# Attention block: the low parts of three value weights computed by VectorE, the other weights still by an adding DMA

## The chip, the cores and the metric

One core of one Trainium2 chip runs the whole kernel. The metric is the device time of one execution in microseconds, as the median of several runs. The engines are called here as in the profile: PE is TensorE (matmuls), PEld its weight loads, DVE is VectorE, ACT is ScalarE, POOL is GpSimd, SP is SyncE, which issues the loads.

## The reference, cut to what matters

One layer of a hybrid backbone over 512 latent and 256 context tokens of width 1024, in float32. Three branches (a gated linear recurrence, differential attention, a gated MLP) read one input projection, are gated, merged and normalised. The change lies in the attention branch, in the projection that gives the values:

```python
px = split_proj(modulate(x, sh_x, sc_x), w_in[l], b_in[l])
...
vx = px[4].reshape(B, T, DIFF_HEADS, DIFF_V_DIM)
k_all = jnp.concatenate([kx, kc], axis=1)
v_all = jnp.concatenate([vx, vc], axis=1)
...
s = jnp.einsum('bqhmd,bkhmd->bhmqk', q.astype(f32), k.astype(f32)) * (DIFF_HEAD_DIM ** -0.5)
p = jax.nn.softmax(s, axis=-1)
w = p[:, :, 0] - lam * p[:, :, 1]
return jnp.einsum('bhqk,bkhe->bqhe', w, v.astype(f32)).astype(v.dtype)
```

There are 8 heads with values of 128 channels each.

## The kernel before, in words

**Split operands.** TensorE multiplies in a rounded float32 format. Each operand is therefore kept as a high part (the value rounded to that format) and a low part (value minus high part), and every product is three matmuls, high by high, high by low and low by high (lines 62, 63 and 64, in `mm3`).

**Weights.** A list `pieces` fixes the order in which 512 KB pieces of weights are loaded and split. SyncE loads a piece into one of three `raw` buffers (`w_dma`). `w_conv` then casts it to the high part on ScalarE (line 133) and makes the low part. In the first and last stages (`state["lo"]` names an engine) VectorE subtracts (line 138). During attention `state["lo"]` is None: ScalarE writes the negated piece, minus `raw`, to the low tile (line 135), and GpSimd issues a DMA that adds the high part's source on top (line 136), so that the low part is what the rounding left over. A raw buffer is free for the next load when its last reader is through.

**Kinds of weights.** Kind `"cm"` is a 128-column block in one piece (keys, queries, gates). Kind `"tm"` is a pair of heads' values, 256 columns in two pieces of 512 rows each, with separate tiles for the high part and the low part. During attention there are three of kind tm: w10, w15 and w20, for head pairs 1, 2 and 3. The pair 0 (w4) is split before attention begins. The names in the rows are these numbers: w15h and w15l are the high and low part of weight 15, raw15_0 and raw15_1 its two pieces.

**Attention.** A loop over 32 steps i, four blocks of 128 queries for each of eight heads. Step i does `scores(i)` (line 729, two matrices s_0 and s_1 in two of three large PSUM buffers), `softmax(i)` (row maxima by VectorE, line 739; exponentials by ScalarE, line 744; a scaling by ScalarE, line 747), and `combine(i)` (VectorE, line 754: the two softmaxes are combined, and the PSUM buffer of s_1 is read for the last time). The transposes of step i-1 (line 759) and their split into wth (ScalarE, line 770) and wtl (VectorE, line 772) follow, and once per head the product with the values (o, lines 62 to 64). Between these, projections for later heads fill TensorE: one projection per step, as written in the table `fill`. The value projections of pair p are the groups v_0 to v_5, one token block of 128 each; their results are split into vh (ScalarE, line 54) and vl (VectorE, line 55).

**Order.** TensorE's instructions stand in the order in which the code is written. The other engines' instructions are put in order by a scheduler that estimates when each can run, and on each engine they run strictly in that order. The first value group of w15 follows the scores of step 13, that of w20 the scores of step 21, that of w10 the scores of step 5.

Of the kernel before, what the change touches and what calls it, by code (L numbers as in the profile page):

```python
# [13 lines left out]
ALU = mybir.AluOpType  # L14
# [15 lines left out]
def block_kernel(ctx, tc, x, c, cctx_in, c_ctx, w_ada, b_ada, w_in, b_in, conv_w, conv_b,  # L30
# [4 lines left out]
    V, S, G, PE = nc.vector, nc.scalar, nc.gpsimd, nc.tensor  # L35

    def f(ap):
        return ap.bitcast(F32)
# [43 lines left out]
    reqs, pieces, raws, parts, last = [], [], {}, {}, {}  # L82
    state = {"dma": 0, "conv": 0, "use": 0, "lo": G, "keep": None, "slot": 0}
# [14 lines left out]
    def w_dma():  # L98
        if state["dma"] >= len(pieces):
            return  # L100
        i, part = pieces[state["dma"]]
        kind, src, c0 = reqs[i][:3]
        if kind == "cm":
            raw = wp.tile([P, KT, P], F32, tag="raw", bufs=3, name=f"raw{i}")
            nc.sync.dma_start(raw, src[:, c0:c0 + P].rearrange("(k p) c -> p k c", p=P))
        elif kind != "tm":
            raw = wp.tile([P, 2, 512], F32, tag="raw", bufs=3, name=f"raw{i}_{part}")
            r0 = 512 * int(kind[1]) + 256 * part
            nc.sync.dma_start(raw, src[r0:r0 + 256, c0:c0 + 512]
                              .rearrange("(k p) c -> p k c", p=P))  # L110
        else:
            raw = wp.tile([P, KT // 2, CW], F32, tag="raw", bufs=3, name=f"raw{i}_{part}")
            nc.sync.dma_start(raw, src[part * 512:part * 512 + 512, c0:c0 + CW]
                              .rearrange("(k p) c -> p k c", p=P))
        raws[state["dma"]] = raw
        state["dma"] += 1

    def w_conv(ahead=True):
        j = state["conv"]
        i, part = pieces[j]  # L120
        kind, slots = reqs[i][0], reqs[i][3]
        if kind == "cm":
            t = wp.tile([P, 2, KT, P], F32R, tag=f"w{slots[0]}", bufs=1, name=f"w{i}")
            parts[i] = (t[:, 0], t[:, 1])
            h, l = parts[i]
        else:
            if part == 0:
                dims = [P, KT, CW] if kind == "tm" else [P, 4, 512]
                parts[i] = tuple(wp.tile(dims, F32R, tag=f"w{sl}", bufs=1, name=f"w{i}{n}")
                                 for sl, n in zip(slots, "hl"))  # L130
            n = parts[i][0].shape[1] // 2
            h, l = (t[:, n * part:n * part + n] for t in parts[i])
        state["hi"] = S.copy(h, raws[j])  # L133
        if state["lo"] is None:
            S.mul(l, raws[j], -1.0)
            G.dma_start(f(l), raws[j], accum_op=ALU.add)  # L136
        else:
            state["lo"].tensor_tensor(l, raws[j], f(h), ALU.subtract)  # L138
        state["conv"] += 1
        if ahead:  # L140
            w_dma()

    def pump(n=1):
        for _ in range(n):
            if state["conv"] >= len(pieces):
                return
            i, part = pieces[state["conv"]]
            if part == 0 and not all(retired(x) for x in reqs[i][4]):
                return
            w_conv()  # L150

    def w_next():
        i = state["use"]
        state["use"] += 1
        while state["conv"] < len(pieces) and pieces[state["conv"]][0] <= i:
            w_conv()
        return parts[i]
# [110 lines left out]
    with tc.tile_pool(name="hd", bufs=1) as hd:  # L268
# [43 lines left out]
        w_dma()  # L312
        state["lo"] = V
        w_conv()
        state["lo"] = G
        load_ada(1)
# [1010 lines left out]
```

## Time and profile before

| | before |
|---|---|
| median of 3 runs | 1010.98 us (1009.31 to 1011.77) |
| the profiled execution's own time | 1007.99 us |
| its span | 1006.2 us |
| TensorE busy, share of the span | 959.5 us, 95% |
| VectorE busy | 629.2 us, 63% |
| ScalarE busy | 553.2 us, 55% |
| GpSimd busy | 107.4 us, 11% |
| mean granted TensorE clock | 0.983 of full speed |

The span is the time from the first to the last instruction in the profile, 1.8 us less than the execution's own time. Busy shares are averages over stages that have different limits; TensorE's 95% still leaves 46.7 us in which it does nothing. The attention loop lies between about 84 and 372 us of the span.

### The profile page before, as it was taken

To read this page: it belongs to the slowest core of one execution; us is meant where nothing else is said; L and a number is where in the kernel's file an instruction comes from. 1 tells how busy PE (TensorE), PEld (TensorE's weight loads), DVE (VectorE), ACT (ScalarE), POOL (GpSimd) and SP (SyncE) were. 2 spreads that over 40 slices of the span, in tenths; PEclk is the share of its full clock that TensorE was granted. 3 is DMA by queue.
4 is the path that set the end of the run, shared out by engine and by line. 5 is a ranking of instruction groups with operands and counts; after the bars stand their busy time and mean duration, and the time that the engine had idled before them with its cause. 6 is when DMAs were issued, how large, how long until landed. Compare 5 with 4: busy or idle time off the path is not lost.

```text
span 1006.2 us, 13286 instructions
## 1 busy us (share of the span) xinstructions
PE 959.5 (95%) x5239; PEld 813.1 (81%) x5239; DVE 629.2 (63%) x996; ACT 553.2 (55%) x771; POOL 107.4 (11%) x118
## 2 busy tenths in 40 slices
PE   5999899989979989999999999999999999999995
PEld 4797779879869868878888887788888888888885
DVE  4468759759758653788778775477333366325566
ACT  4168866757757797998777796333221143332221
POOL 2132122212212121100000000000000000000002
PEclk8999999989989999999999999999999999999998
DMA  9937453362271275222332223734323322845212
GB/s 313 303 101 173 92 139 72 71 152 63 61 170 42 64 159 126 82 74 85 105 94 84 84 76 101 254 109 142 93 75 109 101 84 84 277 140 167 86 41 84
DMA packets 147316, 119.08 MB, mean 118 GB/s; under 512 B 4109, under 2 KB 133622, under 8 KB 147254
## 3 DMA queue, kind: packets, MB, share of 16 engines
q1 hardware_dynamic: 140790, 95.85, 31.5%
q0 software_dynamic: 6320, 22.29, 10.9%
q8 instruction: 41, 0.67, 0.3%
q14 instruction: 21, 0.17, 0.0%
q10 hardware_dynamic: 144, 0.10, 0.0%
HBM read 94.10 MB, written 4.19 MB: 98 GB/s over the span
## 4 chain that ended last, share of the span: by engine, by line
PE 74%; ACT 9%; DVE 9%; DMA 4%; issue 3%; SPq 0%; POOL 0%; POOLq 0%; ACTq 0%; DVEq 0%
PE y L62 4%; PE y L64 4%; PE y L63 4%; PE gt L62 4%; PE gt L64 4%; PE gt L63 4%; PE s L729 3%; DMA raw<-in_w_in_dram 2%; PE out L63 2%; PE out L62 1%; PE out L64 1%; PE v L63 1%; PE gc L62 1%; PE gc L64 1%; PE gc L63 1%
## 5 line engine op out<-in xcount | busy, mean ns | idle before, releaser
L133 ACT CAST w<-raw 128x1024 fp32r<-128x1024 f32 x96 | 99.8, 1044 | 89.6 <-PE y L64 25.3
L138 DVE TENSOR_TENSOR w<-raw,w 128x1024 fp32r<-128x1024 f32 x71 | 86.8, 1229 | 75.2 <-ACT w L133 75.2
L62 PE MATMUL gt<-xhl,w 128*128 128x512 f32 x192 | 75.5, 393 | 0.0
L64 PE MATMUL gt<-xhl,w 128*128 128x512 f32 x192 | 74.8, 390 | 0.0
L63 PE MATMUL gt<-xhl,w 128*128 128x512 f32 x192 | 74.8, 390 | 0.0
L739 DVE TENSOR_REDUCE mxn<-s 128x1 f32<-128x768 f32 x64 | 58.3, 950 | 5.3 <-PE s L729 5.2
L729 PE MATMUL s<-kd,qdq 128*128 128x512 f32 (+1 forms) x256 | 55.6, 358 | 3.0 <-issue 2.8
L729 PEld LDWEIGHTS s<-kd,qdq 128*128 128x128 f32 x256 | 42.9, 191 | 12.7 <-issue 6.3
L62 PEld LDWEIGHTS gt<-xhl,w 128*128 128x128 f32 x192 | 36.1, 188 | 7.6
L64 PEld LDWEIGHTS gt<-xhl,w 128*128 128x128 f32 x192 | 36.0, 188 | 7.7
L63 PEld LDWEIGHTS gt<-xhl,w 128*128 128x128 f32 x192 | 36.1, 188 | 7.1
L744 ACT ACTIVATE e<-s,mxn 128x768 f32<-128x768 f32 x32 | 28.8, 899 | 18.0 <-DVE mxn L739 17.9
L754 DVE SCALAR_TENSOR_TENSOR e<-s,sm,e 128x768 f32<-128x768 f32 x32 | 32.6, 1018 | 7.9 <-ACT e L747 7.1
L1208 POOL PARTITION_BROADCAST grb<-grs x8 | 3.8, 581 | 296.7 <-DVE grs L1205 296.7
L54 ACT CAST vh<-v 128x128 fp32r<-128x128 f32 x48 | 12.3, 265 | 40.5 <-PE v L64 17.8
L772 DVE TENSOR_TENSOR wtl<-t,wth 128x768 fp32r<-128x768 f32 x32 | 30.4, 952 | 6.3 <-ACT wth L770 6.1
L866 ACT ACT_TABLE_LOAD x25 | 32.1, 1283 | 0.4
L747 ACT ACTIVATE e<-e,sm 128x768 f32<-128x768 f32 x32 | 29.9, 936 | 0.4 <-DVE sm L746 0.4
L136 POOL DMA_DIRECT2D w<-raw x24 | 21.5, 907 | 77.0 <-PE s L729 34.3
L866 ACT ACTIVATE rt<-ri,colB 128x770 f32<-128x770 f32 x32 | 28.1, 905 | 2.5 <-PE ri L64 1.4
L744 ACT ACTIVATE s<-s,mxn 128x768 f32<-128x768 f32 x32 | 27.8, 868 | 0.5 <-DVE mxn L739 0.5
L971 POOL DMA_DIRECT2D pa_d<-ha x8 | 4.4, 550 | 220.4 <-DVE ha L970 220.4
(463 smaller groups left out, 3029.2 us busy)
## 6 DMA issues: line engine op xcount, KB each, us to landing
raw<-in_w_in_dram SPq DMA_DIRECT2D x96, 512.0 KB, 4.2
w<-raw POOLq DMA_DIRECT2D x24, 512.0 KB, 4.8
raw<-in_w_branch_dram SPq DMA_DIRECT2D x24, 512.0 KB, 4.0
ada<-in_w_ada_dram SPq DMA_DIRECT2D x6, 1024.0 KB, 8.7
qdq<-qdq POOLq DMA_DIRECT2D x16, 256.0 KB, 5.6
adg<-in_w_ada_dram SPq DMA_DIRECT2D x8, 512.0 KB, 6.3
raw<-in_w_out_dram SPq DMA_DIRECT2D x8, 512.0 KB, 3.6
xtok<-in_x_dram SPq DMA_DIRECT2D x4, 512.0 KB, 5.6
```

The lines of the kernel that those rows point to most:

```text
L62: PE.matmul(ps, ah, bh, start=(first and i == 0), stop=False)
L63: PE.matmul(ps, ah, bl, start=False, stop=False)
L64: PE.matmul(ps, al, bh, start=False, stop=(last and i == n - 1))
L133: state["hi"] = S.copy(h, raws[j])
L138: state["lo"].tensor_tensor(l, raws[j], f(h), ALU.subtract)
L729: PE.matmul(sp[:, sl], qds[h][:, 2 * m + j, qs], kds[h][:, m, sl], start=(j == 0), stop=(j == 1))
L739: V.tensor_reduce(mxn[:, m:m + 1], sps[m][:, 0:TA], mybir.AxisListType.X, ALU.max, negate=True)
L744: S.activation(e, sps[m][:, 0:TA], AF.Exp, bias=mxn[:, m:m + 1], accum_out=sm[:, m:m + 1])
L747: S.mul(es[i][0], es[i][0], sm[:, 0:1])
L754: V.scalar_tensor_tensor(e0, e1, sm[:, 1:2], e0, op0=ALU.mult, op1=ALU.add)
L772: V.tensor_tensor(wts[h][1][:, :, qs], src, f(wts[h][0][:, :, qs]), ALU.subtract)
L866: order[0] = S.activation(out, in_, fn, **kw)
```

## The change

For weights of kind tm during attention, the low part is computed by VectorE as raw minus high part, in one instruction for each piece. Kind cm keeps the negated copy and the adding DMA.

```diff
         state["hi"] = S.copy(h, raws[j])
-        if state["lo"] is None:
+        if state["lo"] is None and kind == "tm":
+            V.tensor_tensor(l, raws[j], f(h), ALU.subtract)
+        elif state["lo"] is None:
             S.mul(l, raws[j], -1.0)
             G.dma_start(f(l), raws[j], accum_op=ALU.add)
         else:
```

This concerns six pieces, two of each of w10, w15 and w20. ScalarE loses six instructions (688 rows of order become 682), GpSimd six DMAs, VectorE gains six. The lines below the change are numbered two higher afterwards (754 becomes 756), and the new instruction is line 135. TensorE's and SyncE's orders keep the same instructions; some of their waits differ.

VectorE's order at step 12, before. The names: s12 and s13 are scores, sm12 the sums, mxn13 the negated maxima, e0_12 the combined softmax, t11 the transposed one, v1_5 the last value group of pair 1, zq4 and t1q4 the query of head 4 on its way through the rotation.

```order
L739 TENSOR_REDUCE mxn12_1956<-s12_1_1950 128x1
L594 TENSOR_TENSOR kd4_1856<-zc4_1888,kd4_1856 64x256
L746 RECIPROCAL sm12_1955<-sm12_1955 128x1
L594 TENSOR_TENSOR kd4_1856<-zc4_1888,kd4_1856 64x256
L55 TENSOR_TENSOR vl2_1300<-v1_5_1904,vh2_1299 128x128
L752 RECIPROCAL sm12_1955<-sm12_1955 128x1
L753 TENSOR_TENSOR sm12_1955<-sm12_1955,nlam_87 128x1
L754 SCALAR_TENSOR_TENSOR e0_12_1958<-s12_1_1950,sm12_1955,e0_12_1958 128x768
L55 TENSOR_TENSOR vl3_1368<-v1_5_1904,vh3_1367 128x128
L545 STREAM_SHUFFLE t1q4_2009<-zq4_1998 128x512
```

The same place of VectorE's order in the changed kernel:

```order
L741 TENSOR_REDUCE mxn12_1952<-s12_1_1946 128x1
L596 TENSOR_TENSOR kd4_1854<-zc4_1886,kd4_1854 64x256
L748 RECIPROCAL sm12_1951<-sm12_1951 128x1
L596 TENSOR_TENSOR kd4_1854<-zc4_1886,kd4_1854 64x256
L55 TENSOR_TENSOR vl2_1298<-v1_5_1902,vh2_1297 128x128
L135 TENSOR_TENSOR w15l_1932<-raw15_0_1400,w15h_1931 128x1024
L754 RECIPROCAL sm12_1951<-sm12_1951 128x1
L55 TENSOR_TENSOR vl3_1366<-v1_5_1902,vh3_1365 128x128
L755 TENSOR_TENSOR sm12_1951<-sm12_1951,nlam_87 128x1
L135 TENSOR_TENSOR w15l_1932<-raw15_1_1622,w15h_1931 128x1024
L756 SCALAR_TENSOR_TENSOR e0_12_1954<-s12_1_1946,sm12_1951,e0_12_1954 128x768
L547 STREAM_SHUFFLE t1q4_2005<-zq4_1994 128x512
```

Both low parts, and vl3, now stand ahead of the combination of step 12. At step 20 (w20) the order has changed in the same way. On ScalarE the cast of the second piece has moved up beside that of the first, into the place of the negated copy.

SyncE's loads around w10, before, with the semaphores each waits for (DMASW is a DMA issued by GpSimd, DMAHW one issued by SyncE):

```order
L113 DMA raw10_1_993<-in_w_in_dram 128x4x256 [waits DMAHW1_49,DMASW7_49,Activation_49]
L105 DMA raw11_1003<-in_w_in_dram 128x8x128 [waits DMAHW2_49,DMASW0_49,Activation_49]
L105 DMA raw12_1249<-in_w_in_dram 128x8x128 [waits DMAHW3_49,DMASW1_49,Activation_49]
L105 DMA raw13_1269<-in_w_in_dram 128x8x128 [waits DMAHW4_49,DMAHW7_49,DMASW2_49,Activation_49]
L105 DMA raw14_1330<-in_w_in_dram 128x8x128 [waits DMAHW0_49,DMAHW5_49,DMASW3_49,Activation_49]
```

The same loads in the changed kernel:

```order
L113 DMA raw10_1_993<-in_w_in_dram 128x4x256 [waits DMAHW1_49,DMASW7_49,Activation_49]
L105 DMA raw11_1003<-in_w_in_dram 128x8x128 [waits DMAHW2_49,DMASW0_49,Activation_49]
L105 DMA raw12_1248<-in_w_in_dram 128x8x128 [waits DMAHW3_49,DVE_49,Activation_49]
L105 DMA raw13_1267<-in_w_in_dram 128x8x128 [waits DMAHW5_49,DMAHW7_49,DMASW1_49,Activation_49]
L105 DMA raw14_1328<-in_w_in_dram 128x8x128 [waits DMAHW4_49,DMAHW0_49,DVE_49]
```

The load of raw12 no longer waits for an adding DMA (that of w10l's first piece) but for VectorE's subtraction of that piece. The load of raw14 now waits for the second subtraction, and raw13 for the adding DMA of w11.

TensorE's scores of step 4, just behind the place where VectorE computes w10l's first piece, before:

```order
L729 MATMUL s4_0_1197<-kd1_738,qdq1_780 128x512 [waits DMASW4_49,DVE_49]
L729 MATMUL s4_0_1197<-kd1_738,qdq1_780 128x512
L729 MATMUL s4_0_1197<-kd1_738,qdq1_780 128x256 x2
L729 MATMUL s4_1_1202<-kd1_738,qdq1_780 128x512 [waits DMASW5_49,DVE_49,PE_49]
L729 MATMUL s4_1_1202<-kd1_738,qdq1_780 128x512
```

And in the changed kernel:

```order
L731 MATMUL s4_0_1197<-kd1_738,qdq1_780 128x512 [waits DMASW4_49,DVE_49]
L731 MATMUL s4_0_1197<-kd1_738,qdq1_780 128x512
L731 MATMUL s4_0_1197<-kd1_738,qdq1_780 128x256 x2
L731 MATMUL s4_1_1202<-kd1_738,qdq1_780 128x512 [waits DMASW5_49,Activation_49]
L731 MATMUL s4_1_1202<-kd1_738,qdq1_780 128x512
```

The scores s4_1 have another PSUM buffer: before, that of s3_1, which the combination of step 3 on VectorE releases; now that of s4_0, which ScalarE's exponential of s4_0 releases. For the scores s13_1 and s21_1 nothing changes here: they wait for the combinations of steps 12 and 20, as before.

## Rows read from the trace of the kernel before

**Rows 1.** The page's part 4: the last-ending chain, its shares by engine.
```profile
PE 74%; ACT 9%; DVE 9%; DMA 4%; issue 3%; SPq 0%; POOL 0%; POOLq 0%; ACTq 0%; DVEq 0%
```
**Rows 2.** The chain of waits in two stretches: start us, length us, what.
```profile
202.72 6.11 DMA w15l<-raw
...
280.57 7.49 DMA w20l<-raw
```
**Rows 3.** TensorE's timeline at w15 and w20; idle time and releaser stand in brackets.
```profile
204.71 0.28 PE L62 MATMUL v<-w15h,xhl 128*128 128x256 f32 x1
208.87 0.58 PE L63 MATMUL v<-w15l,xhl 128*128 128x256 f32 x1 [3.89 <-DMA w15l<-raw]
...
288.11 0.58 PE L63 MATMUL v<-w20l,xhl 128*128 128x256 f32 x1 [5.13 <-DMA w20l<-raw]
```
**Rows 4.** Busy time by window; the number behind POOL's count is the granted clock.
```profile
208.80:214.00 5.20, 5.13 (x18) 4.55 (x19) 4.02 (x9) 1.66 (x4) 1.09 (x2) 0.50 0.98 182
...
288.00:293.00 5.00, 4.89 (x18) 4.42 (x19) 2.48 (x4) 0.27 (x1) 1.08 (x2) 0.54 1.03 232
```
**Rows 5.** The chain of waits at w10: the load of raw12.
```profile
122.86 7.99 DMA raw<-in_w_in_dram
```
**Rows 6.** ScalarE's timeline at w10: the cast of raw12.
```profile
130.93 1.05 ACT L133 CAST w<-raw 128x1024 fp32r<-128x1024 f32 x1 [3.56 <-DMA raw<-in_w_in_dram]
```
**Rows 7.** TensorE's timeline behind the first value group of w10.
```profile
132.72 0.49 PE L62 MATMUL o<-wth,vh 128*128 128x512 f32 x1 [1.15 <-ACT wth L770]
...
139.41 0.38 PE L62 MATMUL v<-w10h,xhl 128*128 128x256 f32 x1 [0.83 <-DVE vl L55]
```
**Rows 8.** VectorE's timeline in a later stage: two subtractions of a piece in succession.
```profile
600.87 2.35 DVE L138 TENSOR_TENSOR w<-raw,w 128x1024 fp32r<-128x1024 f32 x2
```
**Rows 9.** VectorE's timeline at step 12: vl2 and the combination.
```profile
199.60 0.29 DVE L55 TENSOR_TENSOR vl<-v,vh 128x128 fp32r<-128x128 f32 x1
...
201.34 1.02 DVE L754 SCALAR_TENSOR_TENSOR e<-s,sm,e 128x768 f32<-128x768 f32 x1 [0.47 <-ACT e L747]
```
**Rows 10.** TensorE's timeline: the second value groups of w15 and w20 begin.
```profile
217.44 0.38 PE L62 MATMUL v<-w15h,xhl 128*128 128x256 f32 x1
...
296.35 0.39 PE L62 MATMUL v<-w20h,xhl 128*128 128x256 f32 x1
```
**Rows 11.** VectorE's timeline: low parts of the queries (line 571), steps 13 and 21.
```profile
212.34 0.69 DVE L571 SCALAR_TENSOR_TENSOR qdq<-zq,qdq 64x512 fp32r<-64x512 f32 x1
...
288.82 0.67 DVE L571 SCALAR_TENSOR_TENSOR qdq<-zq,qdq 64x512 fp32r<-64x512 f32 x1
```
**Rows 12.** ScalarE's timeline: the casts of raw17 and raw22 behind their loads.
```profile
204.91 1.04 ACT L133 CAST w<-raw 128x1024 fp32r<-128x1024 f32 x1 [1.91 <-DMA raw<-in_w_in_dram]
...
282.31 1.05 ACT L133 CAST w<-raw 128x1024 fp32r<-128x1024 f32 x1 [1.45 <-DMA raw<-in_w_in_dram]
```
**Rows 13.** VectorE's timeline at step 13: the split of t11.
```profile
206.69 0.96 DVE L772 TENSOR_TENSOR wtl<-t,wth 128x768 fp32r<-128x768 f32 x1 [1.22 <-ACT wth L770]
```
**Rows 14.** VectorE's timeline at step 4.
```profile
114.89 0.69 DVE L549 TENSOR_TENSOR zk<-zk,t1k 128x512 f32<-128x512 f32 x1
...
116.59 0.96 DVE L739 TENSOR_REDUCE mxn<-s 128x1 f32<-128x768 f32 x1
```
**Rows 15.** TensorE's timeline at step 4: the scores s4_1.
```profile
118.70 1.62 PE L729 MATMUL s<-kd,qdq 128*128 128x512 f32 x4 [2.76 <-issue]
```
**Rows 16.** ScalarE's timeline at step 4: the exponential of s4_0.
```profile
117.90 0.92 ACT L744 ACTIVATE e<-s,mxn 128x768 f32<-128x768 f32 x1
```
**Rows 17.** Busy time by window, behind two gaps of TensorE.
```profile
118.70:122.00 3.30, 3.30 (x9) 2.72 (x10) 3.15 (x7) 2.75 (x5) 2.25 (x3) 0.50 0.75 149
...
433.00:440.00 7.00, 6.28 (x28) 5.19 (x29) 7.00 (x10) 5.46 (x8) 0.00 (x0) 1.00 0.14 37
```
**Rows 18.** TensorE's timeline: the gap in the second of these windows.
```profile
433.72 0.50 PE L62 MATMUL y<-hsB,w 128*128 128x512 f32 x1 [2.23 <-ACT pad L889]
```
**Rows 19.** The page's part 6: SyncE's loads, count, size, median us to landing.
```profile
raw<-in_w_in_dram SPq DMA_DIRECT2D x96, 512.0 KB, 4.2
```

## The prediction

> **What bounds the kernel now.** I read the views from the outside in. The page's chain that ended last says that TensorE holds 74% of the way to the end and DMAs 4% [rows 1]: a change pays where it ends a wait of TensorE, and an instruction that only leaves ScalarE or GpSimd pays nothing by itself. I then looked for places where TensorE waits for what the change touches. The chain of waits has two of the six adding DMAs in it, w15l's second piece with 6.11 us and w20l's second with 7.49 us [rows 2]. TensorE's own timeline shows what they do: the first value group of w15 runs as far as its 13th matmul at 204.71 and stands for 3.89 us until w15l's second piece has landed; at w20 the same matmul stands for 5.13 us [rows 3]. The reader should also look at the clock behind these gaps: from 208.8 to 214 it is 0.50 and from 288 to 293 0.54 [rows 4], the lower of the two levels, 1.2 GHz. So each gap is paid twice, once as idle time and once as slow matmuls. The two adding DMAs of w10 hold TensorE nowhere directly. But the raw buffer of w10l's first piece is free only when its DMA has landed, so the load of raw12 is issued at 122.86 and takes 7.99 us [rows 5]; ScalarE, which works in order, stands 3.56 us before the cast of raw12 [rows 6], and the cast wth that TensorE needs is queued behind it: 1.15 us of TensorE at 132.72, and a hand-over of 0.83 us at 139.41 at the end of the same chain [rows 7].
>
> **What the two waits cost today.** At w15 TensorE stands for 3.89 us, and in the 5.2 us at half clock behind it does work of 2.6 us, so 2.6 us are lost: 6.5 us together. At w20 it stands for 5.13 us, and the 5.0 us at 0.54 lose 2.3 us: 7.4 us [rows 3, 4]. Both go if the low part is there in time.
>
> **Is it there in time?** The new instruction is the one that line 138 issues in later stages, on tiles of the same size: two in succession take 2.35 us, 1.18 us each [rows 8]. Ahead of step 12's combination VectorE now does vl2, which ends at 199.89 [rows 9], the first low part, three small instructions (a reciprocal, vl3, a product of one column, none longer than vl2's 0.29 us, at most 0.9 together) and the second low part: 199.89 + 1.18 + 0.9 + 1.18 = 203.15. TensorE begins to stand at 208.87 - 3.89 = 204.98 [rows 3]. In time by 1.8 us, and the order at step 20 is the same, so I take both DMA waits as ended. The high parts that the subtraction reads are cast by ScalarE ahead of the exponentials of steps 12 and 20, the second cast in the place of the first negated copy, so the exponentials are not later. The negated copies and the issues on GpSimd lie on the path today only through these waits, and I count nothing more for them: TensorE's matmuls hide them. Without that cover the copies would be worth up to six times 1.05 us, by the cast of the same size [rows 6].
>
> **What is late next.** The combination of step 12 is queued behind the two low parts. It ended at 201.34 + 1.02 = 202.36 [rows 9]; now it runs from 203.15 to 204.2, 1.8 us later at most. The scores s13_1 wait for it, since it frees their PSUM buffer, and before they began without a gap. So TensorE gets a new stall of up to 1.8 us, and another at s21_1. Then the next hand-over. The second value group of w15, at 217.44 [rows 10], would come 6.5 - 1.8 = 4.7 us earlier, at 212.7. But it needs vl5, which stands on VectorE behind the query's second low part, done at 212.34 + 0.69 = 213.03 [rows 11]; that chain hangs on the softmax of step 13 and on the cast of raw17 ahead of it [rows 12], which do not move. With vl5's 0.29 us this makes 213.3: 0.6 us more to wait, and a gain at w15 of **4.1 us**. At w20: 296.35 - 7.4 + 1.8 = 290.75 [rows 10]; VectorE does the query's first low part to 289.5 [rows 11], vl6, the second one and vl7, 289.5 + 0.29 + 0.69 + 0.29 = 290.8: gain **5.6 us**. The product o2 that lies between needs wtl2, done at 206.69 + 0.96 = 207.65 [rows 13]. TensorE comes to it 4.7 us earlier than before with 24 matmuls of the group still ahead of it, at about the same moment, so I count no wait, bound 0.5.
>
> **w10.** VectorE is free for its first low part at 114.89, where it now begins another instruction [rows 14], and is done at 116.1. Then the load of raw12 can be issued, instead of at 122.86. Even with 7.99 us it lands before ScalarE reaches the cast, at 130.93 - 3.56 = 127.4 [rows 5, 6]. So the 1.15 us go, and the 0.83 us most likely with them, since the chain behind the cast (exponentials, combination, vl3) moves up by 3 us. That is 2.0 us of gaps; a second, shorter hold behind the same cast could make it 3.1. I take **2.5 us**. The price: the combination of step 3 comes about 0.8 us later. Before, s4_1 waited for exactly that [rows 15], so it would cost 0.8. Now s4_1 takes the buffer that the exponential of s4_0 frees. The maximum of s4_0 is found after the low part, a reciprocal and the instruction of line 549: 114.89 + 1.18 + 0.29 + 0.69 + 0.96 = 118.0 [rows 14], and the exponential begins at 118.0 instead of 117.90 [rows 16]. I count 0.1, bound 0.8.
>
> **Sum.** 2.4 + 4.1 + 5.6 = 12.1 us. The profiled execution took 1007.99 us (span 1006.2 and 1.8 us around it), which makes 995.9. The median of the runs shown is 3.0 us above that execution; the forecast for a median is 1010.98 - 12.1 = **998.9 us**. Behind the attention loop nothing is bound to an absolute time, so I carry the gain to the end. Bounds of the parts: 1.2 to 3.0 at w10; 3.6 to 4.7 at w15 (the most, if raw17 lands earlier once the adding DMAs are gone); 5.1 to 6.5 at w20. That is 9.9 to 14.2 us, and with 1.5 us for gaps elsewhere that may meet the clock differently the likeliest case reaches from 995.3 to 1002.6.
>
> **A page against the row.** The rows say 6.11 and 7.49 us for the adding DMA of 512 KB [rows 2]. The Trainium skill, "DMA: Bandwidth & Descriptors", section "Anatomy of one DMA — SWDGE (gpsimd) path", gives about 2.0 us fixed plus the bytes over 436 GB/s for a DMA issued by GpSimd, which I estimate at 3.2 us here. By that the pieces would land at 205.9 and 283.8, TensorE would stand for about 1 us each, without a fall of the clock, and the change, which puts up to 1.8 us in their place, would gain nothing at w15 and w20: only the 2.4 us of w10 would remain. The measured holds decide; the trace does not agree with the page here.
>
> **The rivals.**
> *The clock falls in the new stalls too.* A gap of 2.76 us was followed by 3.3 us at 0.50 [rows 15, 17], one of 2.23 us by full clock [rows 17, 18]; the new stalls are shorter than both, but not by far. If it falls as it does now, each place loses about what it loses today, 2.6 and 2.3 us, of which the later wait for vl5 absorbs 0.6: 4.3 us less gain, 7.8 instead of 12.1, median 1003.2. The Trainium skill, "TensorE: Matmul & The Clock Gate", section "HAM oscillation — how this bites in real kernels", says that idle gaps between groups of matmuls throttle the clock if they are long enough; the two rows agree.
> *The loads arrive late.* The raw buffers of w15 and w20 are free earlier, so the loads of raw18 and raw23 start beside those of raw17 and raw22 instead of behind an adding DMA. If raw17 and raw22 then take the 7.99 us of [rows 5] instead of the median of 4.2 [rows 19], all that stands behind their casts [rows 12] comes 3.8 us later, o and vl as well: gain 2.4 + 0.3 + 1.8 = 4.5, median 1006.5.
> *The same, so far that the kernel is slower.* Each microsecond more on these two loads costs two. The gain of 4.5 is gone at loads of 10.2 us, and the kernel is slower by over 3 us from 11.7 us on: 1014 and more. No load that the chain shows takes more than 8.0.
> *The change does not do what it says.* If VectorE reaches the second low part only when the DMA would have landed (6 us later than I reckon, behind a late cast or exponential), the holds stay: about 1009, with w10's gain. Against it: in the trace all that stands ahead of it in the order is done by 202.4 [rows 9].
>
> **How the numbers follow.** Chances: the likeliest case 0.68, the clock 0.16, late loads 0.09, no effect 0.04, slower 0.03. From no change a measurement of this kernel can tell about 0.3%, 3 us (the three runs lie 2.5 us apart). The first three cases are faster: 0.93; same 0.04; slower 0.03. A range of 994.5 to 1005 holds the likeliest and the clock case with their edges and leaves out the late loads and the last two: 0.84 by these chances, less what I may have overlooked.
>
> **What would show it.** Right: no DMA of w15l or w20l as a releaser of TensorE; a gap of up to 1.8 us before s13_1 and s21_1, released by the combination; clock 1.00 in the value groups behind them; both low parts of w15 done before TensorE asks for them; ScalarE without a wait before the cast of raw12; the load of raw12 issued some 7 us earlier. Wrong: a clock of 0.5 behind the new gaps; a load of raw17 or raw22 of 6 us or more; or waits for vl or wtl of over 1 us that eat the gain.

## The result and the profile after

| | before | after |
|---|---|---|
| median of the runs side by side | 1010.68 us (1009.31 to 1011.77, 4 runs) | 998.81 us (997.03 to 999.72, 4 runs) |
| ratio, 95% interval | | 0.9887, 0.9874 to 0.9901 |
| the profiled execution's own time, span | 1007.99, 1006.2 us | 998.82, 996.7 us |
| mean granted TensorE clock | 0.983 | 0.992 |

The change saves 11.9 us; the forecast was 998.9 us. The page's chain that ended last [rows 1] now reads:

```profile
PE 78%; ACT 7%; DMA 6%; DVE 5%; issue 2%; SPq 1%; POOL 0%; POOLq 0%; ACTq 0%; DVEq 0%
```

TensorE's timeline at the places of [rows 3, 7, 10, 15]:

```profile
121.31 1.65 PE L731 MATMUL s<-kd,qdq 128*128 128x512 f32 x4 [3.03 <-ACT e L746]
...
202.84 0.93 PE L731 MATMUL s<-kd,qdq 128*128 128x512 f32 x4 [0.83 <-DVE e L756]
...
212.22 0.39 PE L62 MATMUL v<-w15h,xhl 128*128 128x256 f32 x1 [0.74 <-DVE vl L55]
...
276.20 0.93 PE L731 MATMUL s<-kd,qdq 128*128 128x512 f32 x4 [0.69 <-DVE e L756]
...
285.55 0.39 PE L62 MATMUL v<-w20h,xhl 128*128 128x256 f32 x1 [0.70 <-DVE vl L55]
```

No DMA of w15l or w20l releases TensorE any more. In their place stand a gap before s13_1 and one before s21_1, both released by the combination, and at w15 and w20 a short hand-over to vl. The gaps of w10's chain [rows 7] are gone; the gap at s4_1 is a little longer and is now released by an exponential. The windows behind the new gaps and behind the one at s4_1 (the number behind POOL's count is the granted clock):

```profile
121.30:125.00 3.70, 3.69 (x11) 3.09 (x12) 3.27 (x6) 1.93 (x3) 0.25 (x1) 0.60 0.73 147
202.80:208.00 5.20, 5.16 (x35) 4.83 (x36) 4.25 (x7) 4.86 (x8) 2.18 (x2) 1.00 0.69 194
...
276.20:281.00 4.80, 4.80 (x33) 4.51 (x34) 3.88 (x7) 4.53 (x8) 2.18 (x2) 1.00 0.68 200
```

At w15 and w20 the clock stays at its upper level, 2.4 GHz, where it was 0.50 and 0.54 before [rows 4]. VectorE's timeline at step 12 shows the two low parts and the combination behind them [rows 9]:

```profile
199.09 1.22 DVE L135 TENSOR_TENSOR w15l<-raw,w15h 128x1024 fp32r<-128x1024 f32 x1
...
200.55 1.22 DVE L135 TENSOR_TENSOR w15l<-raw,w15h 128x1024 fp32r<-128x1024 f32 x1
201.68 1.01 DVE L756 SCALAR_TENSOR_TENSOR e<-s,sm,e 128x768 f32<-128x768 f32 x1
```

And ScalarE's timeline shows the casts of raw12 (without a wait) and of raw17 [rows 6, 12], SyncE's the load of raw12 [rows 5]:

```profile
129.72 1.04 ACT L133 CAST w<-raw 128x1024 fp32r<-128x1024 f32 x1
...
203.14 1.05 ACT L133 CAST w<-raw 128x1024 fp32r<-128x1024 f32 x1 [1.76 <-DMA raw<-in_w_in_dram]
```

```profile
118.11 0.37 SPq L105 DMA_DIRECT2D raw<-in_w_in_dram  x1
```

**Where the time came from.** To compare executions that start at different moments I cut each of the 14 traces of this study at TensorE's first matmul of a weight's context group (v from w4h, w10h, w15h, w20h and chl). The cuts of the changed kernel:

```profile
73.63 0.28 PE L62 MATMUL v<-w4h,chl 128*128 128x256 f32 x1
...
174.44 0.37 PE L62 MATMUL v<-w10h,chl 128*128 128x256 f32 x1
...
248.00 0.37 PE L62 MATMUL v<-w15h,chl 128*128 128x256 f32 x1
...
321.25 0.37 PE L62 MATMUL v<-w20h,chl 128*128 128x256 f32 x1
```

The part of w10 is thus 174.44 - 73.63 = 100.81 us long, that of w15 73.56, that of w20 73.25. The cuts in the trace of before:

```profile
72.27 0.28 PE L62 MATMUL v<-w4h,chl 128*128 128x256 f32 x1
...
175.17 0.37 PE L62 MATMUL v<-w10h,chl 128*128 128x256 f32 x1
...
253.20 0.36 PE L62 MATMUL v<-w15h,chl 128*128 128x256 f32 x1
...
332.05 0.36 PE L62 MATMUL v<-w20h,chl 128*128 128x256 f32 x1
```

These make 102.90, 78.03 and 78.85 us. The three parts are shorter by 2.1, 4.5 and 5.6 us, 12.2 together. The two profiled executions differ by 9.2 us only, because the one of after reaches the first cut 1.4 us later and meets half clock later on, for 1.6 us, which no edit touches (last section).

### The profile page after: what moved, and what is told of

Read it like the earlier page. It is cut to its first block, busy times and chain, and to the rows that moved or that the text cites. A ratio compares the mean times of both kernels' runs of the same rounds, so it can differ in the third digit from the quotient of the medians.

```text
span 996.7 us, 13268 instructions
## 1 busy us (share of the span) xinstructions
PE 957.0 (96%) x5239; PEld 810.5 (81%) x5239; DVE 633.6 (64%) x1002; ACT 547.6 (55%) x765; POOL 102.0 (10%) x112
## 4 chain that ended last, share of the span: by engine, by line
PE 78%; ACT 7%; DMA 6%; DVE 5%; issue 2%; SPq 1%; POOL 0%; POOLq 0%; ACTq 0%; DVEq 0%
PE y L62 4%; PE y L63 4%; PE y L64 4%; PE gt L62 4%; PE gt L64 4%; PE gt L63 4%; PE s L731 3%; DMA w<-raw 2%; DMA ada<-in_w_ada_dram 2%; PE v L62 2%; DMA raw<-in_w_in_dram 2%; PE v L63 2%; PE v L64 2%; PE out L63 2%; PE out L62 1%
## 5 line engine op out<-in xcount | busy, mean ns | idle before, releaser
L54 ACT CAST vh<-v 128x128 fp32r<-128x128 f32 x48 | 12.3, 266 | 32.9 <-DVE vl L55 16.2
L62 PE MATMUL y<-hsB,w 128*128 128x512 f32 x64 | 25.8, 404 | 2.7 <-ACT pad L891 2.2
```

Of the source, the lines that this page charges most:

```text
L62: PE.matmul(ps, ah, bh, start=(first and i == 0), stop=False)
```

## The experiments

The 12 runs came in three sets of four, each timed beside before on one chip. A gain is given by the ratio, times the median of before in its set: 1009.08, 1008.93 and 1010.28 us. What the expectations call medians of single runs are gains of this kind.

### One weight at a time (three runs)

```diff
-        if state["lo"] is None and kind == "tm":
+        if state["lo"] is None and i == 10:
```

and the same with 15 and with 20.

> Only w10's two low parts are done by VectorE; those of w15 and w20 keep the negated copy and the adding DMA. My theory (each weight pays by the wait of TensorE that its adding DMA causes): 2.8 us less than before, as in the trace of the changed kernel, about 1007.9; the waits of TensorE for w15l and w20l (3.9 and 5.1 us) stay, with clock 0.5 behind them. Rival (the gain is ScalarE's and GpSimd's work taken away, so it is spread evenly): a third of 11.9 us, 4.0 us less, about 1006.7.

> Only w15's two low parts are done by VectorE. My theory: 4.5 us less than before, about 1006.2; TensorE no longer stands at the 13th matmul of w15's first value group, has a gap of 0.8 us before s13_1 with clock 1.00 behind it, and still stands for 5.1 us at w20. Rival (even spread): 4.0 us less. The two lie too close to be told apart by this run's time alone; it counts beside the runs with w10 alone and w20 alone, and whether the three gains add up to 11.9.

> Only w20's two low parts are done by VectorE. My theory: 5.6 us less than before, about 1005.1, twice the gain of w10 alone; the wait for w15l (3.9 us) and the half clock behind it stay. Rival (even spread): 4.0 us less, about 1006.7.

Measured: w10 1008.70 us, ratio 0.9989 (0.9977 to 1.0000); w15 1006.03, 0.9971 (0.9959 to 0.9982); w20 1005.60, 0.9956 (0.9942 to 0.9971). The gains are 1.1, 2.9 and 4.4 us, in the order of my theory, but each 1.2 to 1.7 us short of it; an even spread of 4 us is refuted by w10 alone, whose interval ends at 2.3 us. The traces did what was expected at their places: with w15 alone TensorE has a gap of 0.83 us before s13_1, and still stands 4.81 us for w20l; the parts were 100.68 us (w10), 73.76 (w15) and 72.99 (w20). Two questions stayed: why the measured gains are smaller than those of the traces, and whether the three pay only together.

### The changed kernel again, before again, a pair, and w10 again (four runs)

> The changed kernel once more, unchanged, beside the others of this set. If the three weights pay independently, as the traces of the single ones say (w10's part of attention 2.9 us shorter, w15's 4.3 to 4.5, w20's 5.1 to 5.6, 12.3 to 13.0 together), it is 11 to 13 us faster than before. If the medians of the single ones (1.1, 2.9 and 4.4 us, 8.4 together) are what each is worth, and nothing is gained by having all three, it is 8.4 us faster, a ratio of 0.9917. And the clock behind the 2.2 us gap at the end of the gate convolution: if it falls in this execution again, that belongs to this kernel; if not, it is chance.

> The kernel before itself, timed against itself: the ratio should be 1.000 and its interval says what a difference of this size is worth. Its trace says how much one execution differs from the next in the stages that no edit touches: the first value weight's start, and the part of attention with w10, which took 102.9 us in the first trace of before and 103.9 and 105.4 in two kernels that leave w10 as it was. By my theory w15's and w20's parts are again 78.0 to 78.9 us long, with waits of 3.5 to 5.5 us for the adding DMAs.

```diff
-        if state["lo"] is None and kind == "tm":
+        if state["lo"] is None and i in (15, 20):
```

> Only the low parts of w15 and w20 are done by VectorE, w10 keeps the adding DMA. If the parts add as the traces have them (4.8 and 5.2 us), it is 10.0 us faster than before, a ratio of 0.990. If each is worth what the medians of the single runs gave (2.9 and 4.4 us), 7.3 us, a ratio of 0.9928, and the rest of the 12.3 us would need all three together.

> The single run of w10 again, on another chip or at another time. By the traces (100.7 against 102.9 to 105.4 us in the part of attention with w10) 3 us faster; by the first measurement 1.1 us. The rival for the difference: the half clock behind the 3.0 us gap at s4_1 lasts longer in some executions than in others, so that the trace of one execution does not tell the median.

Measured: the changed kernel again 996.67 us, ratio 0.9878 (0.9866 to 0.9891); before against itself 0.9986 (0.9972 to 1.0000); the pair 1000.07 us, 0.9896 (0.9875 to 0.9917); w10 again 1007.07 us, 0.9965 (0.9950 to 0.9979).

Before against itself came out 1.4 us too fast: a difference of that size in one set says nothing here, and the gains that fell short in the first set fell short by that much. What made that set low I cannot say. The pair gained 10.5 us and w10 3.5 us, 14.0 together against the 12.3 us of all three. The single ones of the first set came to 8.4. Within what one set can tell the gains add, and nothing shows that it needs all three together. In the trace of before again the holds were 3.75 us (w15) and 4.70 us (w20), and the parts a little shorter than expected. The parts of the traces in which a weight is as in before (adding DMA) or as in the changed kernel (VectorE), in us; a part that another edit changes is given with that edit below:

| part | adding DMA | mean | VectorE | mean | gain |
|---|---|---|---|---|---|
| w10 | 102.90, 103.92, 105.42, 103.76, 104.19 | 104.04 | 100.81, 100.68, 102.69, 100.30, 100.48 | 100.99 | 3.05 |
| w15 | 78.03, 78.76, 78.42, 77.07, 78.81 | 78.22 | 73.56, 73.76, 73.51, 73.73 | 73.64 | 4.58 |
| w20 | 78.85, 78.18, 78.00, 77.90, 78.75 | 78.34 | 73.25, 72.99, 73.24, 73.16 | 73.16 | 5.18 |

The sum is 12.8 us; the two comparisons of the whole change gave 11.4 and 12.3 by their ratios, 11.9 and 12.3 by their medians. At w15 and w20 the two columns do not overlap. At w10 two things widen the columns, and no edit touches the first. Ahead of the scores of step 3 TensorE waits 2.3 to 3.8 us for a vl of the first weight, w4, and this stretch takes 37.4 to 39.3 us in these traces. From step 3 on the columns do not overlap at w10 either: 65.5 to 66.2 us with the adding DMA, 62.5 to 63.8 with VectorE, a gain of 2.9 us. The second is the clock: the same 3.02 us gap at s4_1 was followed by 12 us at 0.86 in one execution and at 0.76 in another, with 60 and 50 matmuls. First w10 alone, then the changed kernel again, each from the end of the gap:

```profile
120.75:132.75 12.00, 12.00 (x60) 10.39 (x61) 10.88 (x20) 5.92 (x9) 2.46 (x3) 0.86 0.54 136
```

```profile
121.45:133.45 12.00, 12.00 (x50) 10.02 (x51) 9.70 (x18) 4.74 (x7) 1.48 (x2) 0.76 0.53 135
```

### The combination ahead of the second low part

```diff
+            def low(l=l, h=h, j=j, late=part and i != 10):
+                if late:
+                    V.tensor_copy(l[:, 0, 0:1], es[max(es)][0][:, 0:1])
+                V.tensor_tensor(l, raws[j], f(h), ALU.subtract)
+            if part and i != 10:
+                defer.append(low)
...
             combine(i)
+        flush()
```

> The changed kernel with the second low parts of w15 and w20 put behind the combination of steps 12 and 20 on VectorE (a copy of one column, taken from the combination's result, holds them there). My theory (the stall at s13_1 and s21_1 is absorbed, since vl5 and vl7 hang on softmax steps whose exponentials stand behind the casts of raw17 and raw22): the gaps of 0.83 and 0.69 us before s13_1 and s21_1 go, and the waits for vl5 and vl7, 0.74 and 0.70 us in the changed kernel, become 1.5 and 1.4 us; the time is that of the changed kernel within 0.3 us. Rival (each stall is lost for good): 1.5 us faster than the changed kernel.

Measured: 996.92 us, ratio 0.9884 (0.9868 to 0.9901), against 996.67 us of the changed kernel in the same set. The gaps before s13_1 and s21_1 are gone. TensorE's timeline at w15:

```profile
206.00 0.50 PE L63 MATMUL o<-wtl,vh 128*128 128x512 f32 x1 [0.56 <-DVE wtl L790]
...
211.70 0.39 PE L62 MATMUL v<-w15h,xhl 128*128 128x256 f32 x1 [0.82 <-DVE vl L55]
```

Most of the 0.83 us came back as 0.56 us at the product, which now waits for wtl2, and as a slightly longer wait for vl5 (0.82 against 0.74). The parts, 73.46 and 73.34 us, are those of the changed kernel. The stall that the change put in costs nothing by itself, since the hand-over behind it hangs on another chain. That it would split into two waits I had not expected.

### Each low part twice

```diff
             V.tensor_tensor(l, raws[j], f(h), ALU.subtract)
+            V.tensor_tensor(l, raws[j], f(h), ALU.subtract)
```

> Each of the six low parts is subtracted twice on VectorE, 1.2 us more at six places; the order changes so that at steps 12 and 20 the first piece is done twice ahead of the combination, the second once behind it and once behind the maxima of the next step, which the product wtl2 and the softmax of that step stand behind. My theory (VectorE's chain is what TensorE waits for at s13_1, s21_1, s4_1 and at the second value groups, so added time there is paid): 1.2 us at w10 and about 2.4 us each at w15 and w20, 6 us slower than the changed kernel, between 3 and 8. Rival (VectorE has idle time, 36% of the span, and added work is hidden): equal to the changed kernel within 0.5 us.

Measured: 1009.58 us, ratio 0.9999 (0.9987 to 1.0012), 12.2 us behind the changed kernel by the ratios. Neither number of mine: added time on VectorE is paid where TensorE comes to wait for it, and there more than I reckoned. The parts of w15 and w20 are 75.99 and 75.62 us, 2.4 and 2.5 us longer, as expected: TensorE stands for 1.41 us behind the 13th matmul of w15, and the wait for vl5 is 1.24 instead of 0.74 us. At s4_1 I was wrong: the gap is still 3.02 us, since only one subtraction stands ahead of it. The rest is w10, 107.20 us. TensorE's timeline there:

```profile
135.79 0.58 PE L63 MATMUL v<-w10l,xhl 128*128 128x256 f32 x1 [3.91 <-DVE w10l L136]
```

and VectorE's, with what it waited for:

```profile
133.39 0.16 DVE L755 RECIPROCAL sm<-sm 128x1 f32<-128x1 f32 x1
133.47 2.27 DVE L136 TENSOR_TENSOR w10l<-raw,w10h 128x1024 fp32r<-128x1024 f32 x1
```

The fourth subtraction stands in VectorE's order behind the softmax of step 5, and runs beside an instruction of GpSimd (1.26 us from 133.40), in 2.27 us instead of 1.2. TensorE stands behind the 13th matmul for 3.91 us, and the 4.2 us that follow run at a clock of 0.50. This is the picture of [rows 3, 4] with VectorE in the DMA's place: what costs is the moment at which the low part is there, not the engine that makes it.

### All six on GpSimd

```diff
-            V.tensor_tensor(l, raws[j], f(h), ALU.subtract)
+            G.tensor_tensor(l, raws[j], f(h), ALU.subtract)
```

> All six low parts as one subtraction each on GpSimd, no negated copy and no DMA; VectorE keeps its order of before. My theory (what pays is that the low part is there in time; what VectorE's version gives back is the stall at s13_1 and s21_1, 0.83 and 0.69 us, since the combinations are queued behind two low parts): both waits for w15l and w20l gone, no gap before s13_1 and s21_1, but the same hand-over of the second value groups to vl5 and vl7, which hangs on the cast of raw17 and raw22; so equal to the changed kernel or up to 1 us faster, 997.8 to 998.8. By the nearest row (2.36 us for such a subtraction on GpSimd) the second low part is done two times 2.36 us after the high parts and in time. Rival (GpSimd's longer instruction holds VectorE up, or is itself late at the 13th matmul): VectorE's instructions beside it take longer by up to 2.36 us at each of the six places, and the time is 1003 or more.

Measured: 1001.54 us, ratio 0.9921 (0.9908 to 0.9934), 3.4 to 4.3 us behind the changed kernel by the ratios. My theory held at w15 and w20 (parts of 73.09 and 72.80 us, no wait for vl5 or vl7, though gaps of 0.95 and 0.81 us before s13_1 and s21_1 stay) and fell at w10 (105.03 us), where the rival was right, though its 1003 us were not reached. The gaps at s13_1 and s21_1 stay because VectorE is held up here too: ahead of the combinations of steps 12 and 20 an instruction on kd, 0.42 us elsewhere, takes 2.31 and 2.32 us beside GpSimd's second piece. TensorE's timeline at w10, then VectorE's and GpSimd's:

```profile
124.26 1.62 PE L731 MATMUL s<-kd,qdq 128*128 128x512 f32 x4 [6.76 <-issue]
```

```profile
116.44 2.67 DVE L551 TENSOR_TENSOR zk<-zk,t1k 128x512 f32<-128x512 f32 x1
119.04 0.15 DVE L754 RECIPROCAL sm<-sm 128x1 f32<-128x1 f32 x1
119.15 2.45 DVE L591 CAST kd<-zk 64x512 fp32r<-64x512 f32 x1
```

```profile
115.95 5.36 POOL L135 TENSOR_TENSOR w10l<-raw,w10h 128x1024 fp32r<-128x1024 f32 x2 [1.40 <-PE kc L64]
```

GpSimd works on two pieces for 2.7 us each, until 118.6 and 121.3. VectorE's product, 0.68 us elsewhere, ends at 119.1, and its cast, 0.42 us elsewhere, at 121.6: each ends 0.3 to 0.5 us after the piece of GpSimd beside it. The maximum of s4_0 behind them begins at 122.15, and TensorE stands 6.76 us for the exponential. The Trainium skill, "SBUF — State Buffer", section "Who interferes with whom", says that VectorE and GpSimd share a pair of ports under an exclusive lock, so that the later one waits and does not merely slow down; these rows agree.

### The adding DMAs earlier

```diff
+        if state["lo"] is None and kind == "tm":
+            with tc.high_priority():
+                state["hi"] = S.copy(h, raws[j])
+                S.mul(l, raws[j], -1.0)
+                G.dma_start(f(l), raws[j], accum_op=ALU.add)
...
```

> The kernel before with one thing changed: negated copies and adding DMAs of the values' weights are put ahead of other ready work, so that at steps 12 and 20 ScalarE does both negated copies ahead of the exponentials and GpSimd can issue the second DMA some 4 us earlier. My theory (what costs is only that the second low part lands late): by the rows of before the second piece would land at about 204.6 instead of 208.87 and the first at 205.3, so that TensorE stands for 2 us at most at w15 instead of 3.89; the exponentials of step 12 come 0.6 to 1.5 us later; 4 to 9 us faster than before. Rival (the adding DMA costs whenever it runs, by its traffic or by GpSimd's issue): the holds stay at 3 to 5 us and the time is that of before within 2 us.

Measured: 1011.07 us, ratio 1.0015 (1.0005 to 1.0026). Nothing was gained; the 1.5 us by which it is slower are about what before differed from itself (1.4). So my theory of a mere lateness is not enough, and the rival was right. TensorE's timeline at w15, then GpSimd's and ScalarE's:

```profile
211.18 0.39 PE L63 MATMUL v<-w15l,xhl 128*128 128x256 f32 x1 [3.05 <-DMA w15l<-raw]
...
222.01 0.39 PE L62 MATMUL v<-w15h,xhl 128*128 128x256 f32 x1 [1.43 <-DVE vl L55]
```

```profile
202.65 1.79 POOL L137 DMA_DIRECT2D w15l<-raw x2 [1.93 <-ACT w15l L136]
```

```profile
212.56 1.05 ACT L142 CAST w<-raw 128x1024 fp32r<-128x1024 f32 x1 [5.93 <-DMA raw<-in_w_in_dram]
```

The two DMAs are issued behind one another, from 202.65 on, and TensorE gets what it waits for at 211.18, over 7 us behind the second issue; it now stands at the second matmul of the group, which needs the first piece. The full clock behind this hold is kept. But the load of raw17, issued at 204.72 beside them, lands only at 212.5, 7.8 us later; in the changed kernel a load issued at 199.14 is there at 203.1. The chains of waits, here and in the changed kernel:

```profile
204.72 7.76 DMA raw<-in_w_in_dram
```

```profile
199.14 3.92 DMA raw<-in_w_in_dram
```

ScalarE stands 5.93 us before that cast, softmax 13 and vl5 come late, and the part stays at 78.14 us. So the adding DMAs cost twice here: by their landing, and by the load beside them. The second is what the prediction's rival of late loads described. It came with adding DMAs and not with other loads alone: in the changed kernel three loads start between 199.1 and 201.8 and land in 3.9 to 4.9 us, and in the next run, which has no adding DMA of a weight in the attention loop, every load there landed in 3.5 to 5.0 us.

### All weights' low parts by VectorE

```diff
-        if state["lo"] is None and kind == "tm":
+        if state["lo"] is None:
```

> All low parts of the attention loop by VectorE, those of the other weights too, so that no adding DMA and no negated copy is left there. My theory (a low part pays on VectorE only where TensorE waited for its DMA; elsewhere it delays the combinations and maxima behind it): slower than the changed kernel by 3 to 12 us, by up to 1.2 us at each of some twenty steps, half of it given back by ScalarE, which has a copy less ahead of the exponentials. Rival (what paid was ScalarE, GpSimd and the DMA queue relieved): faster than the changed kernel, by up to 5 us.

Measured: 1005.49 us, ratio 0.9959 (0.9945 to 0.9972); by the ratios 7 to 8 us behind the changed kernel. The price is where my theory said, on VectorE, but not at the combinations: TensorE has new waits at the second and the context value groups, of 2.6 and 1.2 us at w15, where VectorE comes late to the output of the head before; behind the 2.6 us the clock is 0.64:

```profile
219.69 0.39 PE L62 MATMUL v<-w15h,xhl 128*128 128x256 f32 x1 [2.60 <-DVE ob L782]
...
258.49 0.39 PE L62 MATMUL v<-w15h,chl 128*128 128x256 f32 x1 [1.22 <-DVE ob L782]
```

The parts, 105.86, 78.36 and 78.03 us, are those of before or longer. What was gained at w15 and w20 is given back in full, although ScalarE and GpSimd do less (526.2 and 83.2 us busy, against 547.6 and 102.0). Behind w20 this kernel is 3.7 us faster up to the gate convolution: the gap of 2.63 us before a product with the values, in which TensorE waits for vl in all other traces, is missing. ScalarE's cast vh, which that vl needs, now begins at 364.24, ahead of the exponentials of that step (from 365.62); in the changed kernel it begins at 353.30, behind them (from 350.71), and they stand behind two casts and a negated copy. So work taken from ScalarE came with a gain there. Whether the missing copies or the new order brought it, no run separates.

## Why the prediction was right

- **What bounds the kernel.** Right. The holds at w15 and w20 and the half clock behind them were the price; the change at these weights is worth 4.58 and 5.18 us. ScalarE's negated copies left with the DMAs, and no run keeps the copies and has the low part in time, so their share in this is not measured by itself. That work taken from ScalarE and GpSimd elsewhere pays nothing by itself is not shown: no run takes it away without giving it to VectorE, and with all weights by VectorE the 3.7 us behind w20 came along with it.
- **In time.** Right, with more room than reckoned. The low parts take 1.22 us (1.18 reckoned), but only 0.24 us lie between them (0.9 reckoned for three small instructions), and the second ends at 201.77, when TensorE is still at the scores. ScalarE helped too: with the second cast ahead of both exponentials, the second one no longer has a cast before it, and the combination has no wait of 0.47 us [rows 9].
- **The stall at s13_1 and s21_1.** Right in place and releaser, mis-sized: 0.83 and 0.69 us against at most 1.8. It hardly counts either way, as the run with the combination first shows.
- **The hand-over to vl5 and vl7.** Right: 0.74 and 0.70 us against 0.6 and about 0. This is the step that sets the gain, since it stays where the cast of raw17 puts it. The gain at w15 is 4.58 us against 4.1, since that cast comes 1 us earlier than I had let it (203.14, or 203.9 with the 0.73 us added by which after is ahead at the cut before it, against 204.91): against that cut the load of raw17 begins 0.4 us earlier, and it takes 3.9 us instead of 4.6. The upper bound of 4.7, for a raw17 that lands earlier, was nearer. At w20 the gain is 5.18 us against 5.6, near the lower bound of 5.1; the holds of w20 in the other traces with its adding DMA lie between 4.65 and 5.33 us, so that one trace sized it only to some tenths. In the changed kernel the load of raw17 itself begins when the adding DMA of another weight has landed (from 194.60, 4.48 us), so that one of the adding DMAs that are left stands at the start of this chain.
- **w10.** Right in mechanism: the load of raw12 is issued at 118.11 instead of at 122.86, the cast does not wait, and the gaps behind it are gone. The scores of step 3 begin 2.0 us later in this trace (111.73 against 109.69), so the load comes 6.8 us earlier, as foreseen. The gap at s4_1 grew from 2.76 to 3.03 us, 0.3 us for the 0.1 counted; what that exponential stands behind is a negated copy on ScalarE, up to 120.3, and not the maximum that I followed, which was done at 119.58. The gain is 3.05 us against 2.4, at the upper bound, or 2.9 from step 3 on. A third gap of the same chain went too, which the working had left out: 0.50 us before the product's second matmul, which waited for wtl (133.71 in before).
- **Sum.** 12.1 us, against 12.8 by the parts and 11.9 and 12.3 by the medians. The terms are off by 0.65, 0.5 and -0.4 us and partly cancel; that the median came within 0.1 us of the forecast is luck.
- **The rivals.** The clock did not fall in the new stalls (windows of 1.00). The loads did not come late; raw17's came earlier. A load about as long as I feared (7.8 us) appeared in the attention loop only beside adding DMAs. No effect and slower are out.
- **The Trainium skill against the row.** The row was right: with the holds taken away the gain at w15 and w20 came, 9.8 us together, where the estimate from the Trainium skill, "DMA: Bandwidth & Descriptors", section "Anatomy of one DMA — SWDGE (gpsimd) path", left nothing there.

## What to carry to other kernels

Moving an instruction pays where its result is awaited: move it there alone, for here moving the 24 other pieces as well gave back over half of the gain. Before pricing a stall that a change puts in, follow TensorE to the next hand-over; if that hangs on a chain which the change does not touch, the stall can be absorbed, and so can its removal, as here. Work on GpSimd is not free for VectorE: w10's pieces there held it up for longer than its own subtractions take. By the parts, GpSimd for w15 and w20 with VectorE for w10 would be some 0.9 us better than the changed kernel (0.55 + 0.36); that was not run, and is below what a set here can tell.

## What the runs showed of the hardware

**The same gap meets either clock.** The gap of 2.2 us at the gate convolution [rows 18], far from any edit, stands in all 14 traces. In 10 of them the clock stayed at its upper level behind it (1.00), in 4 it fell to half soon after (0.65 to 0.66 over 4.9 us), and the stretch from this gap to the next one of 1.15 us took 198.6 us instead of 197.0. First the changed kernel, then before again:

```profile
423.10:428.00 4.90, 4.89 (x15) 3.85 (x16) 4.90 (x7) 4.24 (x5) 0.00 (x0) 0.66 0.01 3
```

```profile
433.60:438.50 4.90, 4.89 (x21) 4.05 (x22) 4.90 (x7) 4.24 (x5) 0.00 (x0) 1.00 0.02 3
```

So a comparison of a 2.2 us gap in one trace with a 2.8 us gap in another, as in the first rival, bounds nothing sharply; the hold of 3.05 us with the adding DMAs earlier was followed by full clock at w15 and at w20. Gaps of 0.7 to 0.95 us were followed by full clock in all the traces that had them behind w10's part. The Trainium skill, "TensorE: Matmul & The Clock Gate", section "What's actually happening", says of the start of a kernel that the number of slow matmuls differs between runs of it. The two traces of the changed kernel show the same of this gap: 0.66 in the first, 1.00 in the second.

**The same instruction of VectorE** took 1.2 us alone and 2.27 us beside an instruction of GpSimd of 1.26 us, and its smaller ones 2.4 to 2.7 us instead of 0.4 to 0.7 beside GpSimd's of 2.7 us.
